# One line of 16 steps in the mixer, with each solve issued ahead of the last group's chain and heads

## The chip, the cores and the metric

The kernel runs on one core of a Trainium2 chip. The metric is the device time of one execution in microseconds; lower is better. The time before is 3080.9 us, the median of three runs (3077.79 to 3086.84).

## The reference

The reference is one decoder layer on 2048 tokens of width 1024, in float32. The part that matters here is the mixer. The normed input u is projected by w_in, and the columns go to two groups of heads, whose outputs are put side by side:

```python
u = rms_norm(h, norm_mix); z = u @ w_in
y_m = mlstm_group(z[..., :D_IN_MLSTM], ...)   # 4 heads of 128: conv, silu, chunkwise mLSTM in chunks of 128
y_r = rwkv7_group(z[..., D_IN_MLSTM:], ...)   # 8 heads of 64: a state S (64 x 64) per head, token by token:
#   sa = S a_t;  S = S * w_t + sa b_t + v_t k_t;  y_t = S r_t, then a norm, a bonus term and a gate
h = h + concat([y_m, y_r]) @ w_mix_out
```

After it come a cross-attention into 256 memory tokens, a SwiGLU feed-forward and a last norm. These stages are not touched.

## The kernel before

Every product of float32 values is made of three fp16 products (mm3: high times high, high times low, low times high), accumulated in PSUM. The scheduler of the language orders the instructions: each engine has a queue whose order is fixed when the program is built, by program order as priority and by a simulated time at which each instruction is ready; on the chip each queue runs in that order and waits at its head. A pool with bufs=n hands its n buffers of a tag round; a new tile waits for the last reader of the one whose buffer it takes. `tc.issue_after(ins)` queues what follows on the engine of `ins` behind it.

The mixer (mixer, mixer_pass) runs two passes, hq = 0 and 1, over half of the heads each: two pairs of RWKV heads (e = 0, 1, each 128 partitions wide) and two mLSTM heads. In a pass there are 8 groups (sg) of 256 tokens. A pass first loads and splits its weights: 8 RWKV tiles of three projections (wts[0], tag wh3) and 8 mLSTM tiles of four (wts[1], tag wh4), through wraw buffers of which there are two. Then, for each group:

- load_u: the group's u by DMA (4 tiles of each half, tags uh and ul; 8 buffers, so two groups).
- group: xw by DMA, and a set of buffers (MX, of which there are two; VX, bon and W, two each).
- prepare for e = 0, 1: wps, the projections kps, rps and vps, the decays and keys (KB, RR), the products aps with masks into MX, RR and AY, and the transposes kbps into KBt. bps gives bon, and a second matmul on vps (L385) gives the values VS. RR has four buffers, two groups. Its PSUM tiles come from pax (two banks) and pmm (two banks).
- solve: the triangular blocks of MX go to DRAM (md) and come back as M, and POOL inverts them in 31 steps of two operations (L434, L436). The result goes to DRAM (td, t1d) and comes back as T1 and into MX. Then PE joins the blocks: pps, an ACT copy, xps, an ACT copy into MX. pps and xps take the one bank of psx.
- scan: the state chain over 4 chunks (ch: three matmul stages with ACT copies between, and a DVE step into the next VS), and yps, the output. It returns a tail.
- the tail of the group before: the norm (dq, var, y), tps and gps in the bank of psx, yc, which adds bon and the gate, and the output by DMA.
- mlstm for e = 0, 1: qps twice, the convolution, vops, then skp, ncp and the state Cn; its tail (yt, ymps, ym) is run one head later. In the second pass the heads of the last two groups are held back to the end (late), and their u is loaded again.

Around it, pre_pass fills the first 100 us; after it memory_kv (kvps) and out_proj start as soon as their buffers come free.

Of the kernel before, what the change touches and what calls it, by code (L numbers as in the profile page):

```python
# [7 lines left out]
F32 = mybir.dt.float32  # L8
# [7 lines left out]
P = 128  # L16
# [18 lines left out]
Q0 = 2056  # L35
# [16 lines left out]
def mm3(nc, out, lhs, rhs, start, stop):  # L52
    nc.tensor.matmul(out, lhsT=lhs[0], rhs=rhs[0], start=start, stop=False)  # L53
    nc.tensor.matmul(out, lhsT=lhs[0], rhs=rhs[1], start=False, stop=False)  # L54
    nc.tensor.matmul(out, lhsT=lhs[1], rhs=rhs[0], start=False, stop=stop)  # L55

# [190 lines left out]
def mixer_pass(c, I, hq, tp, T):  # L247

    nc, tc = c.nc, c.tc
    SGN = 256  # L250
    NS = T // SGN
    w_in = I["w_in"][0]
# [3 lines left out]
    wts = [], []  # L256
    for n, o in ((3, Q0), (4, 0)):
        for k in range(KT):
            wk = w_in[k * P:(k + 1) * P, :]
            h = tp.w.tile([P, n * 2 * P], F16, tag=f"wh{n}", name="wh", bufs=8)  # L260
            l = tp.w.tile([P, n * 2 * P], F16, tag=f"wl{n}", name="wl", bufs=8)
            for j in range(0, n, 2):
                m = min(2, n - j)
                raw = tp.x.tile([P, 4 * P], F32, tag="wraw", name="wraw")[:, 0:2 * m * P]
                nc.sync.dma_start(raw.rearrange("p (j c) -> p j c", j=m),
                                  wk[:, o + 512 * j:o + 512 * (j + m)].rearrange("p (j c) -> p j c", j=m)[:, :, 2 * P * hq:2 * P * (hq + 1)])
                s = slice(2 * P * j, 2 * P * (j + m))
                split(nc, h[:, s], l[:, s], raw, c.gmix[:, k:k + 1])
            wts[n - 3].append((h, l))

    st = Ctx()
    st.VS = None
    st.Cn = []
    for e in range(2):
        st.Cn.append(tp.m2.tile([P, P + 1], F32, tag=f"Cn{e}", name="Cn"))
        nc.gpsimd.memset(st.Cn[e], 0.0)

# [13 lines left out]

    def values():
        return tp.sg.tile([P, 2, 4, 2, 64], F32, tag="VS", name="VS")

    def group(sg):
        G = Ctx()
        G.VS = st.VS
        if sg == 0:
            G.VS = values()
            for h in range(2):  # L300
                nc.gpsimd.memset(G.VS[halves[h], :, 0, h], 0.0)
        G.xw = (tp.t2.tile([P, 2, SGN], F16, tag="xw", name="xw"), tp.xz)
        x = [c.l_d[0][i].rearrange("(q p) t -> p q t", q=2)[:, :, sg * SGN:(sg + 1) * SGN] for i in range(2)]
        for b in halves:
            nc.sync.dma_start(G.xw[0][b], x[0])
        nc.sync.dma_start(G.xw[1][b0], x[1])
        G.MX = next(tp.MXs)
        G.VX = tp.sg.tile([P, 2, 4, 2, 64], F32, tag="VX", name="VX")
        G.bon = tp.sg.tile([P, 2, SGN], F32, tag="bon", name="bon")
        G.W = tp.sg.tile([P, 2, 4, 1], F32, tag="W", name="W")  # L310
        return G

    def prepare(sg, e, u, G):
# [10 lines left out]
        VS, VX = G.VS[:, e], G.VX[:, e]  # L324
# [6 lines left out]
        L = tp.t1.tile([P, SGN], F32, tag="L", name="L")  # L331
# [14 lines left out]
        ps = tp.pmm.tile([P, SGN + 1], F32, tag="mm", name="kps")  # L346
# [18 lines left out]
        for h, b in enumerate(halves):  # L365
            nc.vector.scalar_tensor_tensor(RR[b, :, h, 0:64], sq[b], c.kk[b, 0, ct:ct + 1], E[b, :, 0:64],
                                           op0=ALU.mult, op1=ALU.mult)
        kk = tp.t1.tile([P, SGN], F32, tag="kk", name="kk")
        nc.vector.scalar_tensor_tensor(kk, ta, 1.0, k, op0=ALU.add, op1=ALU.mult)
# [40 lines left out]
    def solve(MX, NG):  # L410
# [27 lines left out]
        for e in range(2):  # L438
            nc.sync.dma_start(td.rearrange("q h g u (c e) r -> e (q h g u) c r", e=2)[e], M[NB * e:NB * e + NB, 0:16])
            nc.sync.dma_start(t1d[e].rearrange("h g u r c -> (h g u) r c"), X[NB * e:NB * e + NB // 2])  # L440
        T1 = tp.t1.tile([P, NU, 32], F32, tag="T1", name="T1")
        for h in range(2):
# [8 lines left out]
        lohi = [(slice(64 * h, 64 * h + 32), slice(64 * h + 32, 64 * h + 64)) for h in range(2)]  # L451
        for i in range(NU):
            for h, (a, b) in enumerate(lohi):
                nc.tensor.matmul(pps[b, i], lhsT=MXu[a, i, h, 32:64], rhs=T1[a, i], start=True, stop=True)
        for a, b in lohi:
# [7 lines left out]

    def scan(sg, gs, G):
        y = tp.s2.tile([P, 2, 2, 2, 64], F32, tag="y", name="y")
        st.VS = values() if sg < NS - 1 else None
        for n in range(4):
            ch = tp.psc.tile([P, 2, 3, 64], F32, tag="ch", name="ch")
            for e, g in enumerate(gs):
                for h in range(2):  # L470
                    nc.tensor.matmul(ch[halves[h], e, 0], lhsT=g.RR[:, n, h, 0:64], rhs=G.VS[:, e, n, h], start=True, stop=True)
            R = tp.s2.tile([P, 2, 64], F32, tag="R", name="R")
            nc.scalar.copy(R, ch[:, :, 0])
            for e, g in enumerate(gs):
                nc.tensor.matmul(ch[:, e, 1], lhsT=g.M[:, n].rearrange("p h t -> p (h t)"), rhs=R[:, e], start=True, stop=True)
            for h, b in enumerate(halves):
                nc.scalar.copy(G.VX[b, :, n, h], ch[b, :, 1])
            for e, g in enumerate(gs):
                for h in range(2):
                    last = nc.tensor.matmul(ch[halves[h], e, 2], lhsT=g.KBt[:, n, h], rhs=G.VX[:, e, n, h], start=True, stop=True)  # L480
            dst = G.VS[:, :, n + 1] if n < 3 else st.VS[:, :, 0] if st.VS is not None else None
            if dst is None:
                break
            Sn = tp.s2.tile([P, 2, 64], F32, tag="Sn", name="Sn")
            for h, b in enumerate(halves):
                nc.vector.tensor_tensor(Sn[b], ch[b, :, 2], G.VS[b, :, n, h], ALU.add)
            for h, b in enumerate(halves):
                nc.vector.tensor_tensor(dst[b, :, h], Sn[b], G.W[b, :, n].to_broadcast([64, 2, 64]), ALU.mult)
# [47 lines left out]
    def mlstm(sg, e, u):  # L536
        t0 = sg * SGN
        hp = 2 * hq + e
        m2 = tp.m2
        mb = m2.tile([P, SGN], F32, tag="mb", name="mb")  # L540
        sb = m2.tile([P, SGN], F32, tag="sb", name="sb")
        for i, t in enumerate((mb, sb)):
            nc.sync.dma_start(t, c.m_d[i].rearrange("(h n) t -> h (n t)", h=4)[hp, t0:t0 + SGN].partition_broadcast(P))
        qk = m2.tile([P, 2, SGN], F32, tag="qk", name="qk", bufs=1)
        for j in range(2):
# [7 lines left out]
            for i in range(3):  # L553
                nc.vector.scalar_tensor_tensor(a, z[:, i:i + SGN], cw(i), a, op0=ALU.mult, op1=ALU.add)
            th = m2.tile([P, SGN], F32, tag="th", name="th")
            nc.scalar.activation(th, a, AF.Tanh, scale=0.5)
# [7 lines left out]
        for n in range(2):  # L564
            ts = slice(n * P + 4, (n + 1) * P + 4)
            for k in range(KT):
                h, l = wts[1][k]
                mm3(nc, ps[:, n], (u[k][0][:, ts], u[k][1][:, ts]),
                    [x.rearrange("p (j e d) -> p j e d", j=4, e=2)[:, 2:4, e] for x in (h, l)], k == 0, k == KT - 1)
# [26 lines left out]
        def tail():  # L596
# [5 lines left out]
            nc.vector.reciprocal(r, r)  # L602
            sq = m2.tile([P, 2, P], F32, tag="th", name="msq")
            ss = m2.tile([P, 2], F32, tag="ss", name="ss")
# [4 lines left out]
            nc.vector.scalar_tensor_tensor(r, r, 0.5 * SYM, ss, op0=ALU.mult, op1=ALU.mult)  # L609
            yt = m2.tile([P, 2, P], F32, tag="yt", name="yt", bufs=1)  # L610
            nc.vector.scalar_tensor_tensor(yt, tho, 1.0, num, op0=ALU.add, op1=ALU.mult)
# [24 lines left out]

    mtails, stails = [], []

    def run_mlstm(sg, u):
        for e in range(2):  # L640
            mtails.append(mlstm(sg, e, u))
            if len(mtails) > 1:
                mtails.pop(0)()

    late = []
    for sg in range(NS):
        u = load_u(sg)
        G = group(sg)
        gs = [prepare(sg, e, u, G) for e in range(2)]
        solve(G.MX, 2)  # L650
        stails.append(scan(sg, gs, G))
        if len(stails) > 1:
            stails.pop(0)()
        if hq == 1 and sg >= NS - 2:
            late.append(sg)
        else:
            run_mlstm(sg, u)
    for sg in late:
        run_mlstm(sg, load_u(sg))
    for t in stails + mtails:  # L660
        t()


def mixer(c, I, T):
    tc = c.tc
    with ExitStack() as ctx:
        tp = Ctx()
        for name, bufs, space in (("x", 2, None), ("w", 10, None), ("u", 8, None), ("t2", 1, None),
                                  ("t1", 1, None), ("m2", 2, None), ("k", 2, None), ("sl", 4, None), ("sg", 2, None), ("RR", 1, None), ("s2", 2, None), ("MX", 1, None), ("pmm", 2, PSUM),
# [15 lines left out]
        tc.nc.gpsimd.memset(tp.xz, 0.0)  # L685
        for hq in range(2):
            mixer_pass(c, I, hq, tp, T)

# [748 lines left out]
```

## Time and profile before

| what | us |
|---|---|
| median of 3 runs | 3080.9 |
| the profiled execution | 3079.7 |
| its span, first to last instruction | 3077.9 |
| PE busy | 2907.4 |
| DVE busy | 2099.1 |
| ACT busy | 1210.7 |
| POOL busy | 1143.2 |

The profile is of one execution. Times within it count from the first instruction, in us. PE is the matmul engine, DVE, ACT and POOL the vector, scalar and general engines, SP the queue that issues the DMAs. The 40 slices of the page are 77 us each; the mixer lies in slices 2 to 17. Busy time of PE counts matmuls that overlap one another once. In brackets at the end of a timeline row is the engine's idle time before it and what ended it. The granted clock is a share of 2.4 GHz: 1.00 is full, 0.50 is 1.2 GHz, and a mean over a stretch lies between.

### The profile page before, as it was taken

How to read it: one execution, taken by the hardware profiler on the slowest of the kernel's cores; microseconds unless marked ns; L12 is line 12 of the kernel's file. 1: busy time of each engine (PE TensorE's matmuls, PEld its weight loads, DVE VectorE, ACT ScalarE, POOL GpSimd, SP SyncE). 2: the span in 40 equal slices, each digit the busy share in tenths (PEclk: the TensorE clock that was granted, in tenths of full speed). 3: DMA queues.
4: the chain of work that ended last, by engine and by line, in shares of the span. 5: the costliest groups of instructions: out<-in, count | busy, mean ns of one | idle time of the engine just before them, and what ended most of it. 6: DMA issues, size and time to landing. Idle time of an engine off the chain costs nothing. (4 is left out here: it accounts for less than half of the span.)

```text
span 3077.9 us, 53602 instructions
## 1 busy us (share of the span) xinstructions
PE 2907.4 (94%) x20259; PEld 1806.3 (59%) x20259; DVE 2099.1 (68%) x3821; ACT 1210.7 (39%) x2763; POOL 1143.2 (37%) x1862
## 2 busy tenths in 40 slices
PE   7799999989999978999999999999999999899998
PEld 4588788778888867765455544444444444344443
DVE  5676677787777766665488897554445455897975
ACT  6444433454444434554366653222222222423332
POOL 2144555555445554033112234222222221644542
PEclk9899999999999988999999999999999999999999
DMA  8612211242122212564323356211111112554442
GB/s 270 143 48 51 55 47 44 57 124 52 47 62 52 52 45 84 179 201 148 110 86 124 109 203 212 73 58 55 55 55 55 59 59 63 178 188 145 155 141 76
DMA packets 333181, 309.34 MB, mean 101 GB/s; under 512 B 89102, under 2 KB 282876, under 8 KB 332028
## 3 DMA queue, kind: packets, MB, share of 16 engines
q1 hardware_dynamic: 332924, 305.94, 32.4%
q8 instruction: 159, 2.61, 0.3%
q14 instruction: 98, 0.80, 0.1%
HBM read 210.36 MB, written 95.49 MB: 99 GB/s over the span
## 5 line engine op out<-in xcount | busy, mean ns | idle before, releaser
L53 PE MATMUL pp<-u,wb 128*128 128x512 f16 x1232 | 467.5, 379 | 14.2 <-DVE e L1142 9.4
L54 PE MATMUL pp<-u,wb 128*128 128x512 f16 x1232 | 467.7, 380 | 0.0
L55 PE MATMUL pp<-u,wb 128*128 128x512 f16 x1232 | 467.3, 380 | 0.0
L1142 DVE TENSOR_TENSOR e<-pp,e 128x512 f32<-128x512 f32 x308 | 208.6, 689 | 303.1 <-PE pp L55 290.2
L55 PE MATMUL dps<-w,gS 128*128 128x512 f16 x616 | 233.4, 379 | 10.8 <-DVE gS L49 10.8
L54 PE MATMUL dps<-w,gS 128*128 128x512 f16 x616 | 233.5, 379 | 1.7 <-DVE w L49 1.7
L53 PE MATMUL dps<-w,gS 128*128 128x512 f16 x616 | 233.5, 379 | 0.0
L434 POOL TENSOR_TENSOR tmp<-M,X 64x126 f32<-64x126 f32 (+22 forms) x496 | 187.2, 377 | 116.3 <-DMA M<-md 82.7
L436 POOL TENSOR_TENSOR X<-X,tmp 64x126 f32<-64x126 f32 (+22 forms) x496 | 202.4, 408 | 35.7
L54 PEld LDWEIGHTS <-wb 128*128 128x128 f16 x1232 | 120.6, 98 | 156.3 <-issue 12.4
L53 PEld LDWEIGHTS <-wb 128*128 128x128 f16 x1232 | 120.7, 98 | 150.9 <-DMA u<-u_d 5.4
L55 PEld LDWEIGHTS <-wb 128*128 128x128 f16 x1232 | 120.7, 98 | 146.0 <-issue 0.7
L1158 POOL TENSOR_TENSOR S<-raw 128x512 f32<-128x512 f32 x22 | 33.0, 1500 | 413.7 <-DVE wb L49 413.7
L53 PE MATMUL vops<-wh,uh 128*128 128x256 f16 x512 | 144.5, 282 | 8.4 <-ACT cv L552 8.1
L53 PE MATMUL qps<-uh,wh 128*128 128x259 f16 x512 | 144.8, 283 | 4.6 <-ACT wh L48 2.8
L54 PEld LDWEIGHTS <-wh 128*128 128x128 f16 x1280 | 128.6, 101 | 28.6 <-issue 8.1
L55 PE MATMUL vops<-wh,ul 128*128 128x256 f16 x512 | 144.5, 282 | 0.0
L54 PE MATMUL vops<-wl,uh 128*128 128x256 f16 x512 | 144.1, 282 | 0.0
L55 PE MATMUL qps<-uh,wl 128*128 128x259 f16 x512 | 143.6, 282 | 0.2 <-DVE wl L49 0.2
L54 PE MATMUL qps<-ul,wh 128*128 128x259 f16 x512 | 143.7, 281 | 0.0
L53 PEld LDWEIGHTS <-wh 128*128 128x128 f16 x1280 | 127.6, 100 | 22.3 <-ACT wh L48 3.7
L55 PEld LDWEIGHTS <-wl 128*128 128x128 f16 x1280 | 127.2, 99 | 20.4 <-DVE wl L49 0.9
(420 smaller groups left out, 7657.3 us busy)
## 6 DMA issues: line engine op xcount, KB each, us to landing
g_d<-e SPq DMA_DIRECT2D x88, 256.0 KB
h<-h_d SPq DMA_DIRECT2D x32, 512.0 KB
acc<-h_d SPq DMA_DIRECT2D x32, 512.0 KB
u_d<-ub SPq DMA_DIRECT2D x56, 256.0 KB
wraw<-in_w_in_dram SPq DMA_DIRECT2D x48, 256.0 KB
ga<-g_d SPq DMA_DIRECT2D x32, 384.0 KB
raw<-in_ffn_w_gate_dram SPq DMA_DIRECT2D x22, 512.0 KB
raw<-in_ffn_w_up_dram SPq DMA_DIRECT2D x22, 512.0 KB
```

Source lines behind the costliest of these rows:

```text
L53: nc.tensor.matmul(out, lhsT=lhs[0], rhs=rhs[0], start=start, stop=False)
L54: nc.tensor.matmul(out, lhsT=lhs[0], rhs=rhs[1], start=False, stop=False)
L55: nc.tensor.matmul(out, lhsT=lhs[1], rhs=rhs[0], start=False, stop=stop)
L434: nc.gpsimd.tensor_tensor(tv, M[:, s, s + 1:32].unsqueeze(2).to_broadcast(shp), X[:, s, 0:ncl].unsqueeze(1).to_broadcast(shp), ALU.mult)
L436: nc.gpsimd.tensor_tensor(X[:, s + 1:32, 0:ncl], X[:, s + 1:32, 0:ncl], tv, ALU.add)
L1142: add = lambda o, x, y: nc.vector.tensor_tensor(o, x, y, ALU.add)
L1158: nc.gpsimd.tensor_tensor(s[0], a[1][0], a[1][1], ALU.add)
```

## The change

mixer_pass no longer runs its pass. It returns its parts, and mixer makes one line of 16 steps of the two passes. In step i a group is prepared; the join of group i-1 is issued; the solve of group i is issued up to its DMAs back to DRAM; then come the scan of group i-1, its first mLSTM head, its tail, and its second head. The solve is cut in two: solve (to td and t1d) and join (T1, MX, pps, xps). The pps matmuls of join(i-1) are queued behind the last vops matmul of mlstm(i-2). The RWKV weights of a pass are loaded ahead of its first preparation and the mLSTM weights after that step; u is loaded a step ahead, with 12 buffers. VS is allocated in group; a scan writes the next group's VS (NX). mb, sb, th and y go from two buffers to one, yt takes the tag of kt and kk that of L. The late heads are gone.

```diff
 def mm3(nc, out, lhs, rhs, start, stop):
...
-    nc.tensor.matmul(out, lhsT=lhs[1], rhs=rhs[0], start=False, stop=stop)
+    return nc.tensor.matmul(out, lhsT=lhs[1], rhs=rhs[0], start=False, stop=stop)
...
     wts = [], []
-    for n, o in ((3, Q0), (4, 0)):
+
+    def weights(i):
+        n, o = ((3, Q0), (4, 0))[i]
         for k in range(KT):
...
     def group(sg):
         G = Ctx()
-        G.VS = st.VS
+        G.VS = tp.sg.tile([P, 2, 4, 2, 64], F32, tag="VS", name="VS")
         if sg == 0:
-            G.VS = values()
...
-        kk = tp.t1.tile([P, SGN], F32, tag="kk", name="kk")
+        kk = tp.t1.tile([P, SGN], F32, tag="L", name="kk")
...
             nc.sync.dma_start(t1d[e].rearrange("h g u r c -> (h g u) r c"), X[NB * e:NB * e + NB // 2])
+        return MXu, NU, td, t1d
+
+    def join(MXu, NU, td, t1d, after):
+
         T1 = tp.t1.tile([P, NU, 32], F32, tag="T1", name="T1")
...
-        for i in range(NU):
-            for h, (a, b) in enumerate(lohi):
-                nc.tensor.matmul(pps[b, i], lhsT=MXu[a, i, h, 32:64], rhs=T1[a, i], start=True, stop=True)
+        with tc.issue_after(after.ins) if after is not None else nullcontext():
+            for i in range(NU):
+                for h, (a, b) in enumerate(lohi):
+                    nc.tensor.matmul(pps[b, i], lhsT=MXu[a, i, h, 32:64], rhs=T1[a, i], start=True, stop=True)
...
-    def scan(sg, gs, G):
-        y = tp.s2.tile([P, 2, 2, 2, 64], F32, tag="y", name="y")
-        st.VS = values() if sg < NS - 1 else None
+    def scan(sg, gs, G, NX):
+        y = tp.s2.tile([P, 2, 2, 2, 64], F32, tag="y", name="y", bufs=1)
...
-            dst = G.VS[:, :, n + 1] if n < 3 else st.VS[:, :, 0] if st.VS is not None else None
+            dst = G.VS[:, :, n + 1] if n < 3 else NX.VS[:, :, 0] if NX is not None else None
...
-        mb = m2.tile([P, SGN], F32, tag="mb", name="mb")
-        sb = m2.tile([P, SGN], F32, tag="sb", name="sb")
+        if sg == 0:
+            st.Cn[e] = m2.tile([P, P + 1], F32, tag=f"Cn{e}", name="Cn")
+            nc.gpsimd.memset(st.Cn[e], 0.0)
+        mb = m2.tile([P, SGN], F32, tag="mb", name="mb", bufs=1)
+        sb = m2.tile([P, SGN], F32, tag="sb", name="sb", bufs=1)
...
-            th = m2.tile([P, SGN], F32, tag="th", name="th")
+            th = m2.tile([P, SGN], F32, tag="th", name="th", bufs=1)
...
-                mm3(nc, ps[:, n], (u[k][0][:, ts], u[k][1][:, ts]),
+                st.last = mm3(nc, ps[:, n], (u[k][0][:, ts], u[k][1][:, ts]),
...
-            yt = m2.tile([P, 2, P], F32, tag="yt", name="yt", bufs=1)
+            yt = m2.tile([P, 2, P], F32, tag="kt", name="yt", bufs=1)
...
-    for sg in range(NS):
-        u = load_u(sg)
-        G = group(sg)
-        gs = [prepare(sg, e, u, G) for e in range(2)]
-        solve(G.MX, 2)
-        stails.append(scan(sg, gs, G))
-        if len(stails) > 1:
-            stails.pop(0)()
-        if hq == 1 and sg >= NS - 2:
-            late.append(sg)
-        else:
-            run_mlstm(sg, u)
-    for sg in late:
-        run_mlstm(sg, load_u(sg))
...
-        for hq in range(2):
-            mixer_pass(c, I, hq, tp, T)
+        NS = T // 256
+        steps = [(p, sg) for p in [mixer_pass(c, I, hq, tp, T) for hq in range(2)] for sg in range(NS)]
+        mtails, us, after = [], {}, None
+
+        def run(i, NX):
+
+            nonlocal after
+            p, sg = steps[i]
+            tail = p.scan(sg, gs[i], G[i], NX)
+            for e in range(2):
+                mtails.append(p.mlstm(sg, e, us[i]))
+                if e == 0:
+                    tail()
+                if len(mtails) > 1:
+                    mtails.pop(0)()
+            after = p.st.last
+
+        G, gs, tri = {}, {}, {}
+        for i, (p, sg) in enumerate(steps):
+            if sg == 0:
+                p.weights(0)
+            if i == 0:
+                us[0] = p.load_u(0)
+            if i + 1 < len(steps):
+                us[i + 1] = steps[i + 1][0].load_u(steps[i + 1][1])
+            G[i] = p.group(sg)
+            gs[i] = [p.prepare(sg, e, us[i], G[i]) for e in range(2)]
+            if i > 0:
+                p.join(*tri[i - 1], after)
+            tri[i] = p.solve(G[i].MX, 2)
+            if i > 0:
+                run(i - 1, G[i] if sg > 0 else None)
+            if sg == 0:
+                p.weights(1)
+        steps[-1][0].join(*tri[len(steps) - 1], after)
+        run(len(steps) - 1, None)
```

## Rows read from the trace of the kernel before

**Rows 1.** The page's first part: busy time of each engine, share, instructions.

```profile
PE 2907.4 (94%) x20259; PEld 1806.3 (59%) x20259; DVE 2099.1 (68%) x3821; ACT 1210.7 (39%) x2763; POOL 1143.2 (37%) x1862
```

**Rows 2.** The page's second part: PE's busy tenths in 40 slices.

```profile
PE   7799999989999978999999999999999999899998
```

**Rows 3.** Windows at groups' first projections: start, end, length, then busy time per engine.

```profile
core 0: us, PE busy (x) PEld busy (x) DVE busy (x) ACT busy (x) POOL busy (x), PEclk, DMA share, GB/s
377.00:445.00 68.00, 64.74 (x675) 55.46 (x674) 49.06 (x119) 27.85 (x85) 34.35 (x82) 0.95 0.21 50
511.00:577.00 66.00, 62.33 (x677) 54.01 (x677) 49.53 (x120) 27.89 (x86) 35.45 (x90) 1.00 0.21 53
577.00:651.00 74.00, 65.29 (x680) 55.88 (x679) 56.58 (x131) 37.33 (x99) 34.89 (x82) 0.98 0.35 87
651.00:724.00 73.00, 65.11 (x659) 54.09 (x657) 60.08 (x138) 37.64 (x103) 40.76 (x86) 0.98 0.40 102
308.00:1051.00 743.00, 695.18 (x7316) 598.01 (x7315) 556.86 (x1326) 323.85 (x955) 391.53 (x914) 0.98 0.24 59
```

**Rows 4.** PE's waits, 100 to 1300 us: total us, times, longest us.

```profile
PE pps L454 <- DMA T<-t1d: 43.4, 18, 6.2
PE wps L330 <- ACT KBt L407: 10.3, 9, 7.4
```

**Rows 5.** Timeline, 393 to 485 us: start, duration, engine, line, operation, tiles, count.

```profile
393.41 1.12 DVE L366 SCALAR_TENSOR_TENSOR RR<-sq,kk,E 64x256 f32<-64x256 f32 x2
...
417.34 0.31 PE L454 MATMUL pps<-T,MX 32*32 32x32 f32 x2 [2.38 <-DMA T<-t1d]
...
424.85 0.73 ACT L462 COPY MX<-xps 32x256 f32<-32x256 f32 x2 [1.87 <-PE xps L460]
...
428.12 0.61 PE L514 MATMUL tps<-ident,y 128*128 128x128 f32 x4
...
429.93 0.69 DVE L526 TENSOR_TENSOR yc<-yc,bon 128x512 f32<-128x512 f32 x1
...
431.69 0.42 DVE L382 TENSOR_TENSOR bon<-bps,v 128x256 f32<-128x256 f32 x1
...
432.14 0.47 ACT L288 ACTIVATE v<-vps,mu_c 128x256 f32<-128x256 f32 x1 [1.45 <-DVE bon L382]
...
440.90 0.43 DVE L399 TENSOR_TENSOR MX<-aps,mask 64x256 f32<-64x256 f32 x1
...
444.17 0.39 ACT L570 ACTIVATE vx<-vops 128x256 f32<-128x256 f32 x1
...
485.06 0.24 PE L454 MATMUL pps<-T,MX 32*32 32x32 f32 x2 [2.33 <-DMA T<-t1d]
```

**Rows 6.** Timeline, 491 to 530 us: the start and the end of group 4's chain.

```profile
491.14 0.73 ACT L462 COPY MX<-xps 32x256 f32<-32x256 f32 x2 [1.07 <-PE xps L460]
...
529.07 0.29 PE L495 MATMUL yps<-VS,RR 128*64 128x64 f32 x4
```

**Rows 7.** Windows at the start and at the end of the mixer.

```profile
100.00:181.00 81.00, 60.92 (x516) 48.99 (x513) 51.99 (x130) 37.29 (x85) 9.15 (x33) 0.83 0.44 89
1051.00:1240.00 189.00, 158.68 (x1615) 134.95 (x1614) 120.46 (x287) 74.09 (x216) 98.37 (x233) 0.87 0.28 75
```

**Rows 8.** Timeline of ACT and PE around 145 us.

```profile
144.35 0.72 ACT L48 ACTIVATE wh<-wraw,gmix 128x512 f16<-128x512 f32 x1 [8.17 <-DMA wraw<-in_w_in_dram]
...
145.89 0.37 PE L330 MATMUL wps<-xw,lwa 128*128 128x256 f16 x1 [7.44 <-ACT KBt L407]
```

**Rows 9.** Timeline of SP: the first load of u for group 1.

```profile
177.97 0.38 SPq L633 DMA_DIRECT2D uh<-u_d  x1
```

**Rows 10.** Waits of all engines, 236 to 1051 us.

```profile
ACT th L556 <- DVE cv L554: 31.2, 33, 3.2
...
ACT wh L48 <- DMA wraw<-in_w_in_dram: 28.9, 21, 3.7
```

**Rows 11.** Groups of PE instructions by line, 1229 to 1283 us: count, busy us, mean ns.

```profile
L54 PE MATMUL kvps<-memT,wk 128*128 128x256 f16 x128 | 35.6, 278 | 0.0
```

More of the change, by code (lines that the diff above doesn't have):

```diff
@@ L250, in mixer_pass @@
     SGN = 256
-    NS = T // SGN
     w_in = I["w_in"][0]
@@ L268, in mixer_pass @@
                 split(nc, h[:, s], l[:, s], raw, c.gmix[:, k:k + 1])
-            wts[n - 3].append((h, l))
+            wts[i].append((h, l))
     st = Ctx()
[L272 to L276, printed above, removed]
+    st.Cn = [None, None]
     def project(ps, j, e, u):
@@ L290, in shifted @@
         return o
-    def values():
-        return tp.sg.tile([P, 2, 4, 2, 64], F32, tag="VS", name="VS")
     def group(sg):
         G = Ctx()
-        G.VS = st.VS
+        G.VS = tp.sg.tile([P, 2, 4, 2, 64], F32, tag="VS", name="VS")
         if sg == 0:
-            G.VS = values()
             for h in range(2):
@@ L602, in tail @@
             nc.vector.reciprocal(r, r)
-            sq = m2.tile([P, 2, P], F32, tag="th", name="msq")
+            sq = m2.tile([P, 2, P], F32, tag="th", name="msq", bufs=1)
             ss = m2.tile([P, 2], F32, tag="ss", name="ss")
@@ L635, in load_u @@
         return u
[L637 to L645, printed above, removed]
-    for sg in range(NS):
-        u = load_u(sg)
-        G = group(sg)
-        gs = [prepare(sg, e, u, G) for e in range(2)]
-        solve(G.MX, 2)
-        stails.append(scan(sg, gs, G))
-        if len(stails) > 1:
-            stails.pop(0)()
-        if hq == 1 and sg >= NS - 2:
-            late.append(sg)
-        else:
-            run_mlstm(sg, u)
-    for sg in late:
-        run_mlstm(sg, load_u(sg))
-    for t in stails + mtails:
-        t()
+    p = Ctx()
+    p.weights, p.load_u, p.group, p.prepare, p.solve, p.join, p.scan, p.mlstm, p.st = \
+        weights, load_u, group, prepare, solve, join, scan, mlstm, st
+    return p
 def mixer(c, I, T):
@@ L667, in mixer @@
         tp = Ctx()
-        for name, bufs, space in (("x", 2, None), ("w", 10, None), ("u", 8, None), ("t2", 1, None),
+        for name, bufs, space in (("x", 2, None), ("w", 10, None), ("u", 12, None), ("t2", 1, None),
                                   ("t1", 1, None), ("m2", 2, None), ("k", 2, None), ("sl", 4, None), ("sg", 2, None), ("RR", 1, None), ("s2", 2, None), ("MX", 1, None), ("pmm", 2, PSUM),
@@ L685, in mixer @@
         tc.nc.gpsimd.memset(tp.xz, 0.0)
-        for hq in range(2):
-            mixer_pass(c, I, hq, tp, T)
+        NS = T // 256
[31 more added lines that the diff above has]
+        run(len(steps) - 1, None)
+        for t in mtails:
+            t()
 def out_proj(c, I, T):
```

## The prediction

> **What bounds the kernel now.** I read the page's first two parts, then the mixer cut into its steps, then what PE waited for, and last one turn of the largest wait. Every time below is made against the profiled execution: 3079.7 us, of which 1.8 lie around the span of 3077.9. The median of the runs is 1.2 above it.
>
> PE is busy for 94% of the span and no other engine for more than 68% [rows 1]. The slices show PE full from the 18th on, so only the mixer, from about 100 to 1285 us, has something to give [rows 2].
>
> Cut at the first projection of each group, a group away from the pass boundary takes 66 to 68 us. At clock 1.00 PE has 62.3 us of work in 66, at 0.95 it has 64.7 in 68; the two groups at the boundary take 74 and 73 [rows 3]. PE sets the pace, with some 3.5 us idle per group. Most of this has one owner: PE waits 43.4 us for T1, the solve's result that comes back by DMA. The next wait, wps with 10.3, belongs mostly to the start [rows 4].
>
> One turn of that wait [rows 5]. T1 of group 3 is there and pps starts at 417.34; ACT writes the joined MX at 424.85. Only then does tps of group 2's tail run, at 428.12: it takes the one psx bank, and the program gives it to pps and xps first. yc adds bon at 429.93, which frees that buffer, so group 4's bon is written at 431.69; this frees v, which ACT shifts for head 1 at 432.14. The last MX of the group follows at 440.90. The solve runs on POOL, and pps of group 4 finds T1 at 485.06. From pps to pps this is 67.7 us, one step. So each solve waits for the join of the solve before it: a loop through one step, beside a PE that has 62 us of work in it.
>
> **The change part by part.**
>
> *The order.* In the trace the chain of group 4 already runs from MX at 491.14 to yps at 529.07 [rows 6], that is beside the preparation of group 5 and the start of group 6, whose step begins at 511 [rows 3]. Much of the overlap that the new order writes out is there, made by the planner. New are two things. tail(i) is issued in its own step, ahead of the next join, so tps no longer stands behind that join on psx. And prepare(i) is ahead of scan(i-1) and mlstm(i-1).
>
> The loop through bon now spans two steps: last MX to pps 44.2 (485.06 - 440.90), pps to MX written 8.2 (425.58 - 417.34), chain 37 (491.9 to 529.1), yps to the release of bon, and from there to the last MX 10 (441.3 - 431). Of the fourth term tps to yc is 2.5; even 20 for it leaves 119 for two steps, 60 for one, below PE's 62.
>
> Another loop stays. RR, VS and MX have two sets, so RR of group i waits for the chain of group i-2. RR of head 0 at 393.41 to the last MX at 440.90 is 47.5 [rows 5]; with 44.2, 8.2 and 37 it makes 137 for two steps, 68 for one. The 47.5 hold the wait for bon, which goes; I expect 35, and so 62 for one step. This leaves no room to speak of below PE.
>
> *A. The wait at pps.* The last solve has nothing to hide behind, so of 18 gaps one of the mean size, 2.4, stays; at most -41 goes. At least nothing: pps is queued on PE where the planner believes T1 to be, the chip needs 44.2 us from the last MX, and the edge to the last vops of group i-2 moves pps only if that comes later. ACT takes group 4's last vops at 444.17, just as its preparation ends [rows 5]; with the heads a step later this lies beside the end of prepare(5), and T1 still needs its 44. The edge alone does not reach. I take half, -20, because the loop is cut but the place in PE's queue is not.
>
> *B. The clock.* The granted clock over the eleven groups from 308 to 1051 is 0.98, so 15 us of 743 [rows 3]; the lower steps have the longer gaps. Bounds 0 and -15; it goes with the waits, by half, -7.
>
> *C. The start.* From 100 to 181 PE is busy 60.9 of 81 at 0.83 [rows 7]: 20 idle, and up to 14 for the clock. ACT was held 8.17 by one weight load, and behind it stood the KBt copy and wps [rows 8]; u for group 1 was issued only at 177.97 [rows 9]. Now u(1) is loaded ahead, and prepare(1) is issued ahead of mlstm(0), whose weights come last. The first solve and chain still pass bare. Bounds 0 and -25; I take -12, near the 10.3 of wps plus part of the clock.
>
> *D. The pass boundary.* 147 us for two groups against 132: 15 too long [rows 3]. ACT waited 28.9 us for weight loads there [rows 10]. The RWKV weights can now load when prepare(7) is through, a step ahead of their use. The mLSTM weights still wait for mlstm(7), and are wanted after prepare(9) and the chain; with 16 loads that cover may be too short, and then PE stands as before. Bounds 0 and -15; -8.
>
> *E. The end.* From 1051 to 1240 PE is idle 30.3 of 189 at 0.87 [rows 7]. Before, the heads of groups 14 and 15 were held back for the last chains; now those of 14 lie beside solve(15), and those of 15 beside what is left, nearly the same. The last chain is covered by the kvps matmuls, of which one of three lines, 128 each, is at work for 35.6 us [rows 11]; they want the mLSTM weights out of the way. If the heads run out before solve(15) is back, up to +15 is bare; if the joins of 13 and 14 no longer stall, up to -25 goes. I take -6.
>
> *F. Fewer buffers.* mb, sb, th and y lose one, yt takes kt's, kk takes L's. The next mb is queued on SP behind the readers of the last one, and behind it on SP stand md, t1d and T1, which have more room than before. kt of the next head waits for the transposes of yt. Where a single buffer is handed round already, th from cv, ACT waits 31.2 us in 33 for it, off PE's path [rows 10]. Bounds 0 and +25, nearer the first; +4. The 16 reloads of u for the two held-back groups go, and nothing waited for them: 0. The memsets of Cn, VS allocated in group() and the return value of mm3 move beside a busy PE: 0. If that cover is gone, a memset or two at the start.
>
> Sum: -20 - 7 - 12 - 8 - 6 + 4 = -49. 3079.7 - 49 = 3030.7, and with the 1.2 to the median 3032.
>
> One rule speaks against the change. The Trainium skill, "Perfetto Trace Analysis", section Identifying the Most-Contended Engine, says that a gap which repeats on the engine that should be full can mean that there is too little SBUF or PSUM for the next tile. The change adds no PSUM bank and takes SBUF buffers away, so by this rule A and B would be nothing. The trace agrees by half: the wait ends on a DMA, but what makes the DMA late is the single psx bank.
>
> **The rivals.** *The wait stays* (24%). The planner had overlapped the chain already, and queues pps where it believes T1 to be; A and B are nothing, and the edges count: -12 - 8 - 6 + 4 = -22, so 3059. For it: the place of the chain in the trace, and 44 us from MX to pps as before. Against it: the loop through psx and bon is cut.
>
> *All of it goes* (11%): -41 - 15 - 20 - 13 - 12 + 4 = -97, so 2984. For it: the bon loop falls below PE's work. Against it: the RR loop near 62.
>
> *Slower* (12%). prepare(i) ahead of scan(i-1) stretches the chain, for which RR, VS and MX of group i+1 wait. At 68 per step this loop is as long as a step now. Each microsecond added to it costs half of one in each of some 13 steps, 6.5 in all. If head 0 to last MX does not shrink and the chain grows by 10, that is +65, and with the edges +43, so 3124. It decides from a net growth of 3.4 us (22 / 6.5). For it: 68 against 66. Against it: the 47.5 hold the wait for bon.
>
> *Nothing moves* (3%): the edges and new waits cancel, 3081.
>
> **How the numbers follow.** The forecast has 50%, with 3000 to 3060 as its own range. From 2985 to 3080 the range holds the forecast, nearly all of the first rival and half of the second; outside lie the other half of it and the slower case. A measurement of this kernel tells 0.3%, some 9 us, from no change. Faster: the forecast, 11% and 19 of the first rival's 24, 80% in all; the same: its other 5 and the 3, 8%; slower: 12%.
>
> **What would show it.** Right: PE's wait at pps falls from 43 to about 20; tps of a group starts ahead of the next group's pps; the last MX comes earlier in its step; steps of 63 to 65 us; the boundary's two groups below 140; PE busy for over 68 of the first 81 us. Wrong: pps waits 2.3 in each step as before (the first rival); or PE waits at ch, aps or kps for VS, RR or the copies, and steps are above 67 (the slower one).

## The result, and the profile after

The changed kernel takes 3048.6 us (median of 4 runs, 3046.7 to 3052.1), the kernel before 3083.9 beside it: ratio 0.9888, 95% interval 0.9867 to 0.9910, some 35 us faster. The forecast was 3032, with 3000 to 3060 as its own range: the direction came, and about two thirds of the gain. The wait that the change was to cut fell as forecast; the idle time of PE hardly did. The profiled execution is the slowest of the four, 3052.1 with a span of 3050.4, so the two profiles lie only 27.5 us apart; the accounts below add up to that. Of the six executions of b_tail below one took 6010.6 us, which no run explains; its median counts it, its ratio does not.

The page's first part and PE's slices, to be held against [rows 1, 2]:

```profile
PE 2888.4 (95%) x20259; PEld 1798.7 (59%) x20259; DVE 2097.6 (69%) x3821; ACT 1213.9 (40%) x2763; POOL 1134.6 (37%) x1862
PE   7779999998999998999999999999999999899998
```

PE's waits of after, 100 to 1300 us (total us, times, longest us), for [rows 4]:

```profile
PE qps L53 <- DVE r L286: 19.5, 13, 2.2
PE qps L53 <- ACT cv L552: 10.9, 13, 0.8
...
PE pps L452 <- DMA T<-t1d: 5.6, 3, 4.2
```

The wait for T1 fell from 43.4 to 5.6. But two waits at qps, the first projection of an mLSTM head, hold 30.4 now; before, they were below 5. Windows of after, cut as [rows 3] at groups' first projections (start, end, length, busy times, clock, DMA); the first three are steady groups (away from the pass boundary), the next three the boundary, the last the same eleven groups as 308 to 1051 before:

```profile
359.00:423.00 64.00, 61.33 (x669) 53.53 (x667) 48.36 (x119) 28.07 (x85) 33.52 (x82) 1.00 0.21 52
423.00:488.00 65.00, 61.68 (x673) 54.01 (x671) 49.12 (x119) 28.70 (x87) 34.32 (x84) 1.00 0.21 53
488.00:552.00 64.00, 60.92 (x666) 53.34 (x664) 48.40 (x118) 27.92 (x85) 34.32 (x86) 1.00 0.22 51
552.00:622.00 70.00, 64.31 (x651) 55.20 (x650) 54.48 (x127) 34.10 (x94) 34.37 (x83) 0.93 0.32 85
622.00:692.00 70.00, 64.85 (x697) 56.58 (x696) 52.27 (x129) 32.26 (x97) 37.99 (x91) 1.00 0.26 61
692.00:764.00 72.00, 63.74 (x653) 54.22 (x651) 56.12 (x127) 35.42 (x92) 37.09 (x79) 0.95 0.36 91
296.00:1022.00 726.00, 682.37 (x7318) 593.77 (x7317) 551.79 (x1326) 326.61 (x954) 381.87 (x911) 0.99 0.24 60
```

The eleven groups went from 743 to 726. Of these 17 us only 4 are idle time of PE (743 - 695.2 = 47.8 before, 43.6 now); 13 are busy time, of the same matmuls. By the granted clocks, 0.98 of 743 us and 0.99 of 726, the lower clock took some 15 us before and some 7 now (17 and 9 where the windows are cut finer). So some 8 of the 13 are the clock; the other 5 are busy time that no run explains.

The ends are to be taken together, since the line leaves work of the start for the end (2084 and 2064 matmuls before; 1845 and 2321 now). First two rows before, then two after:

```profile
60.00:308.00 248.00, 218.70 (x2084) 175.98 (x2083) 169.32 (x402) 114.07 (x295) 82.03 (x209) 0.92 0.38 95
1051.00:1283.00 232.00, 201.15 (x2064) 171.43 (x2063) 149.38 (x355) 101.37 (x283) 101.05 (x235) 0.90 0.33 92
```

```profile
60.00:296.00 236.00, 194.60 (x1845) 156.13 (x1844) 154.22 (x352) 104.43 (x258) 86.01 (x213) 0.89 0.38 98
1022.00:1257.00 235.00, 217.12 (x2321) 187.71 (x2319) 168.10 (x406) 112.66 (x321) 101.28 (x238) 0.97 0.31 86
```

Together 480 became 471, again not by idle time (60.2 and 59.3) but by busy time (419.9 and 411.7); by the clocks shown, the lower clock took some 43 us of them before and some 33 now. With the eleven groups this is 26 of the 27.5 us: 5 idle, 21 busy, and of these some 18 the clock.

One step of after, for [rows 5] (start, duration, engine, line, operation, tiles, count; in brackets the idle time before and its releaser). First the end of group 3's chain, beside the preparation of group 5:

```profile
442.31 0.63 DVE L313 MEMSET RR<- 64x256 f32 x2 [0.76 <-PE ch L468]
...
446.27 0.29 PE L492 MATMUL yps<-VS,RR 128*64 128x64 f32 x4
...
446.54 0.61 DVE L483 TENSOR_TENSOR Sn<-ch,VS 64x128 f32<-64x128 f32 x2 [2.11 <-ACT VX L474]
...
447.18 0.62 DVE L485 TENSOR_TENSOR VS<-Sn,W 64x128 f32<-64x128 f32 x2
...
447.83 0.96 DVE L371 TENSOR_TENSOR RR<-r,E 64x256 f32<-64x256 f32 x2
...
448.83 0.47 ACT L285 ACTIVATE r<-rps,mu_c 128x256 f32<-128x256 f32 x1 [2.90 <-DVE RR L371]
...
449.34 0.48 DVE L286 SCALAR_TENSOR_TENSOR r<-rps,mu_s,r 128x256 f32<-128x256 f32 x1 [0.54 <-ACT r L285]
...
449.87 0.27 PE L53 MATMUL qps<-uh,wh 128*128 128x259 f16 x1 [1.34 <-DVE r L286]
```

This is the new wait. RR of head 0 stands on DVE behind the chain's last step. It is the last reader of r, so ACT can't write the next r; rps keeps its bank, and qps, which is queued for that bank, stops PE for 1.34. The first row is the loop through RR of the prediction: RR of group 5 is not written before the chain of group 3 has read that part of the same buffer for the last time. Then the tail and the join:

```profile
454.74 1.64 POOL L506 TENSOR_TENSOR var<-var,mhalf 128x8 f32<-128x8 f32 x1
...
458.21 1.06 POOL L507 TENSOR_TENSOR y<-y,var 128x512 f32<-128x512 f32 x1
...
459.33 0.66 PE L511 MATMUL tps<-ident,y 128*128 128x128 f32 x4 [1.15 <-POOL y L507]
...
466.46 0.69 PE L452 MATMUL pps<-T,MX 32*32 32x32 f32 x32
```

tps of group 3 is now ahead of pps of group 4. pps comes 50.0 us after the last MX of its group (416.48), where the way through the solve took 44 before, and has nothing to wait for. In place of 2.4 us at pps the step has 1.34 here, 0.84 behind cv, and 1.15 at tps: 3.3 us of idle, as before the change.

### The profile page after: what moved, and what is told of

Same layout as the page of the kernel before. It is cut to its first block, busy times and chain, and to the rows that moved or that the text cites. A ratio compares the mean times of both kernels' runs of the same rounds, so it can differ in the third digit from the quotient of the medians.

```text
span 3050.4 us, 53575 instructions
## 1 busy us (share of the span) xinstructions
PE 2888.4 (95%) x20259; PEld 1798.7 (59%) x20259; DVE 2097.6 (69%) x3821; ACT 1213.9 (40%) x2763; POOL 1134.6 (37%) x1862
## 5 line engine op out<-in xcount | busy, mean ns | idle before, releaser
L1173 POOL TENSOR_TENSOR S<-raw 128x512 f32<-128x512 f32 x22 | 33.8, 1536 | 410.8 <-DVE wb L49 410.8
L53 PE MATMUL qps<-uh,wh 128*128 128x259 f16 x512 | 144.5, 282 | 30.4 <-DVE r L286 19.5
```

What stands on the lines that cost most here:

```text
L1173: nc.gpsimd.tensor_tensor(s[0], a[1][0], a[1][1], ALU.add)
```

## The experiments

Each kernel is made of the one before or of the changed one by the diff shown. The table has the median, the ratio to the kernel before with its interval, and for the same eleven groups of the profiled execution their length, PE's idle time in it, and the clock. The profiled execution of a_tailY is the slowest of its twelve, 3078.0.

| kernel | us | ratio | groups | idle | clock |
|---|---|---|---|---|---|
| before | 3077.6 to 3083.9 | 1 | 743 | 47.8 | 0.98 |
| after | 3048.6 | 0.9888 (0.9867 to 0.9910) | 726 | 43.6 | 0.99 |
| b_tail | 3020.9 | 0.9804 (0.9783 to 0.9824) | 694 | 21.4 | 1.00 |
| b_bon3 | 3055.9 | 0.9924 (0.9905 to 0.9942) | 733 | 43.7 | 0.98 |
| b_tail_one | 3044.3 | 0.9883 (0.9863 to 0.9903) | 722 | 33.8 | 0.98 |
| b_tail_wraw3 | 3023.4 | 0.9816 (0.9796 to 0.9836) | 702 | 23.9 | 0.99 |
| a_noedge | 3049.4 | 0.9904 (0.9887 to 0.9921) | 724 | 44.8 | 1.00 |
| a_tailY | 3069.2 | 0.9966 (0.9953 to 0.9979) | 745 | 42.4 | 0.97 |
| a_solvelate | 3054.2 | 0.9919 (0.9902 to 0.9935) | 731 | 47.2 | 0.99 |
| a_two | 3068.7 | 0.9964 (0.9948 to 0.9979) | 740 | 48.8 | 0.97 |
| a_mbsb | 3052.2 | 0.9911 (0.9898 to 0.9925) | 726 | 42.7 | 0.99 |
| a_ytth | 3053.4 | 0.9919 (0.9906 to 0.9933) | 724 | 41.0 | 0.99 |
| a_full8 | 3068.5 | 0.9965 (0.9953 to 0.9978) | 736 | 49.5 | 0.99 |
| a_half10 | 3065.1 | 0.9957 (0.9943 to 0.9971) | 735 | 48.7 | 0.99 |

**b_tail**: of the change, only this in the kernel before: a group's tail is issued after its own first mLSTM head, ahead of the next join.

```diff
             mtails.append(mlstm(sg, e, u))
+            if e == 0 and stails:
+                stails.pop(0)()
...
         stails.append(scan(sg, gs, G))
-        if len(stails) > 1:
-            stails.pop(0)()
```

> The kernel before with one thing of the change: a group's tail is issued behind its own first mLSTM head, ahead of the next group's join, in place of one group later behind that join. Theory (the one psx bank): this alone cuts the loop pps - MX - tps - bon - v - last MX - solve - pps; the wait at pps falls from 43 to under 20 and the time by 15 to 30, to 3054 to 3069. Rival (the gain comes from preparing a group and issuing its solve ahead of the last group's chain and heads): the wait stays at about 40 and the time within 6 us of the kernel before.

The eleven groups' window, and the head of PE's waits, 100 to 1300 us:

```profile
303.00:997.00 694.00, 672.63 (x7327) 588.28 (x7326) 552.73 (x1327) 321.74 (x956) 381.13 (x914) 1.00 0.26 63
```

```profile
PE pps L454 <- DMA T<-t1d: 11.9, 5, 4.4
```

And the largest of PE's waits in the eleven groups:

```profile
PE tps L514 <- POOL y L510: 5.5, 7, 1.8
```

This one move gives 60 us, more than the whole change. No wait takes the place of the one at pps within the groups; of the wait's 11.9 us, 11.0 lie behind them, at the end. In the groups tps of the tail runs ahead of the next pps here too, on the bank they share. A steady group takes 60 to 63 us. It is the fastest version of all, and it beats both kernels with intervals apart.

**b_bon3**: the kernel before with three bon buffers.

```diff
-        G.bon = tp.sg.tile([P, 2, SGN], F32, tag="bon", name="bon")
+        G.bon = tp.sg.tile([P, 2, SGN], F32, tag="bon", name="bon", bufs=3)
```

> The kernel before with three buffers for bon in place of two, order untouched. Theory (the loop runs through bon): group i's bon no longer waits for the tail of group i-2, v is free earlier, the last MX of a group comes some 10 us earlier in its step, the wait at pps falls to under 25 and the time by 10 to 25, to 3059 to 3074. Rival (bon's wait is beside the path, and PE's queue order alone makes the wait at pps): wait and time as in the kernel before, within 6 us.

```profile
PE pps L454 <- DMA T<-t1d: 23.8, 12, 3.1
```

With the tail still late, a third buffer alone takes 20 of the 43.4 off the wait and 24 us off the time. But only 10 of the 24 lie in the eleven groups, and there the wait goes on:

```profile
PE pps L454 <- DMA T<-t1d: 18.8, 8, 3.1
```

The last MX comes 56 us into its step (370.2 to 426.1) instead of 64, so the loop through bon is cut, and yet pps of that group is queued earlier too and waits 2.07 at 471.53. Room for bon shows the loop; the early tail shows that it is the order on the bank of psx that ends the wait in steady groups.

**a_tailY**: the changed kernel with tps and gps in the bank of yps instead of psx.

```diff
-            tps = tp.psx.tile([P, 2, SGN], F32, tag="sx", name="tps")
+            tps = tp.psc.tile([P, 2, SGN], F32, tag="Y", name="tps")
...
-        gps = tp.psx.tile([P, 2, SGN], F32, tag="sx", name="gps")
+        gps = tp.psc.tile([P, 2, SGN], F32, tag="Y", name="gps")
```

> The kernel after with the tail's tps and gps in the bank of yps, which is free between two groups, in place of psx. Theory (the one psx bank): in the kernel after the steps of 64.3 us are a loop chain - tail - psx free - pps - xps - chain (yps of group 3 at 448, tps 459.3, gps read at 463.6, pps 466.5, MX 472.6, yps of group 4 at 512), while PE has 61 us of work in a step; T1 has landed some 8 us before pps starts. Without the bank between them pps starts when T1 is there, steps go to 61.5 to 63 and the time to 3015 to 3032. A part may come back as a wait of pps for T1 of 1 to 2 us a step. Rival (PE's work with its short waits sets 64.3): no change, 3043 to 3053.

Slower by 20 to 24 (by medians or by ratios), where I expected faster or the same. The waits, 100 to 1300 us:

```profile
PE pps L452 <- DMA T<-t1d: 33.6, 19, 4.3
```

Freed of the shared bank, pps is queued on PE ahead of the tail in some turns (398.77, with tps at 406.38) and waits there for T1; I read this as the place where the planner believes T1 to be, too early for the chip. In the change it is psx, given to tps and gps of the group before, that puts pps behind them, past the landing of T1. The loss is not idle time in the groups, though (42.4, and 43.6 in the change): their busy time is 20 us longer, at a clock of 0.97.

**a_noedge** (`after = None`, so pps isn't tied to the last vops) and **a_solvelate** (solve(i) issued behind run(i-1)) undo one edit of the line each:

```diff
-            tri[i] = p.solve(G[i].MX, 2)
             if i > 0:
                 run(i - 1, G[i] if sg > 0 else None)
+            tri[i] = p.solve(G[i].MX, 2)
```

> The kernel after without the edge that queues pps behind the last vops of the group before last. Theory (the one psx bank): in the kernel after pps of group 4 starts at 466.46, 43 us behind the last vops of group 3 (423), and right behind the tail of group 3, whose tps and gps hold the bank; so the edge is idle and the time stays within 5 us of the kernel after, 3043 to 3053, with a wait at pps of some 6 us in all. Rival (the edge is what keeps pps from waiting): the wait at pps comes back with 2 to 2.5 us a step, over 30 us in all, and the time is 3070 to 3085.

> The kernel after with the solve of group i issued behind the scan, heads and tail of group i-1 in place of ahead of them; all else as in the kernel after. Theory (the tail's POOL operations stand behind the solve's): in the kernel after var of group 3 is ready at 452.7 and its power runs on POOL at 454.74, behind the copies and the memset of solve 4, and an affine_select of 1.78 lies between it and the y product; so yps to tps takes 11.3 us (448.0 to 459.3) against 8 in the kernel before with the early tail, and the loop chain - tail - psx - pps - chain is 64.3 in place of 61. With the solve behind, steps go to 61 to 62.5 and the time to 3010 to 3030. Rival (the single buffers, or preparing ahead of the chain, cost the kernel after its 28 us against the early tail alone): 3043 to 3053 as before the edit.

Neither moves the time clear of the noise. The edge is idle (the last vops of group 3 ends at 423, pps of group 4 starts at 466). a_solvelate does not settle its theory, that the tail's POOL operations stand behind the solve's: in its profile POOL's queue is still in that order, with the solve's affine_select still between the tail's power (386.35) and its product, and yps to tps takes 12 us as before the edit (379.39 to 391.21; 382.29 to 394.33 in the change):

```profile
387.96 1.78 POOL L421 TENSOR_SCALAR_AFFINE_SELECT X<-X 32x512 f32<-32x512 f32 x2
389.82 1.06 POOL L507 TENSOR_TENSOR y<-y,var 128x512 f32<-128x512 f32 x1
```

**a_two**: the changed kernel with the line cut at the pass boundary, so that group 7 is joined and run before group 8 is prepared.

```diff
+            if sg == 0 and i > 0:
+                steps[i - 1][0].join(*tri[i - 1], after)
+                run(i - 1, None)
             if sg == 0:
                 p.weights(0)
...
-            if i > 0:
+            if sg > 0:
```

> The kernel after with its line cut at the pass boundary: join and scan, heads and tail of group 7 are issued ahead of the second pass's weights and of the preparation of group 8. Theory (the line hides nothing at the boundary: the three groups there take 74, 65 and 73 us in the kernel after, 19 over three steps of 64.3, and waiting for weights is the cause, whatever the order): within 10 us of the kernel after, 3043 to 3058. Rival (the line hides solve and chain of group 7 behind group 8): 20 to 40 us slower, 3068 to 3090.

Three groups at the boundary, first here, then in the change:

```profile
554.00:776.00 222.00, 197.73 (x1983) 168.59 (x1980) 162.24 (x380) 101.12 (x281) 110.18 (x251) 0.93 0.31 76
```

```profile
552.00:764.00 212.00, 192.90 (x1996) 166.00 (x1995) 162.87 (x382) 101.78 (x282) 109.45 (x252) 0.96 0.31 80
```

It costs 20 to 23. In the profiles, 17 us apart, 10 lie at the boundary and 4 in the other eight groups. So the theory, that the line hides nothing there, fell. In this order the line is needed at the boundary; against the kernel before, whose three groups take 208, it gains nothing there.

**b_tail_one** and **b_tail_wraw3**: b_tail with the change's single buffers (y aside), and with three wraw buffers.

```diff
-        mb = m2.tile([P, SGN], F32, tag="mb", name="mb")
+        mb = m2.tile([P, SGN], F32, tag="mb", name="mb", bufs=1)
...
-            yt = m2.tile([P, 2, P], F32, tag="yt", name="yt", bufs=1)
+            yt = m2.tile([P, 2, P], F32, tag="kt", name="yt", bufs=1)
...
```

> The kernel before with the early tail (3021) and with the change's single buffers: mb, sb, th one each, yt in kt's place, kk in L's. Theory (fewer buffers cost next to nothing): 3019 to 3029. Rival (the fewer buffers are what makes the kernel after slower than the early tail alone): 3038 to 3050.

> The kernel before with the early tail (3021) and three buffers for the raw weights in place of two. Theory (start and boundary wait for the weight loads, two in flight at a time): ACT's wait for wraw falls by a third, the two groups at the boundary, 67 and 74 us against 61, come near 63 to 68, and the time is 3005 to 3016. Rival (the loads' own rate, or the splits on ACT and DVE, set it): 3017 to 3026.

The buffers cost 24 us in this order; more room for the weights gives nothing. 12 of the 28 us that the groups lose are idle time of PE, 16 busy time, most of it the clock (0.98 of 722 us, 14).

**a_mbsb**, **a_ytth**, **a_full8**, **a_half10**: the buffers given back to the changed kernel, in two parts, and together. All together need room: a_full8 has 8 u tiles and loads u behind run(i-1); a_half10 has 10, y single, and loads half of u early.

```diff
-        mb = m2.tile([P, SGN], F32, tag="mb", name="mb", bufs=1)
-        sb = m2.tile([P, SGN], F32, tag="sb", name="sb", bufs=1)
+        mb = m2.tile([P, SGN], F32, tag="mb", name="mb")
+        sb = m2.tile([P, SGN], F32, tag="sb", name="sb")
...
-            if i + 1 < len(steps):
-                us[i + 1] = steps[i + 1][0].load_u(steps[i + 1][1])
```

> The changed kernel with two buffers each for mb and sb alone, the mLSTM head's rows that SP loads. Theory A: these are the single buffers that cost (SP's queue stands 70 us behind their readers in eight steps): half or more of the 24 us come back, 3022-3037. Theory B: the cost is in th, yt and kk: 3043-3053.

> The changed kernel with two th buffers and yt in a tile of its own instead of kt's. Theory A (mb and sb cost): 3043-3053. Theory B (ACT and DVE wait for each other over th and kt, between one head's end and the next group's start): half or more of the 24 us come back, 3022-3037.

> The changed kernel with every buffer of before restored (mb, sb, th, y two each; yt and kk in tiles of their own), paid for by 8 instead of 12 u tiles, so the loads of group i+1's u are issued behind run(i-1) instead of ahead of prepare(i). Theory: the single buffers cost about 24 us here as they do in the kernel of before with the early tail; steps fall from 64.3 to 62-63 us and the time to 3015-3035. Rival 1: what holds this kernel at 64 us a step is its order (a group prepared ahead, banks in another order), not the buffers: 3042-3055. Rival 2: u arrives late by 4 tiles less, and PE waits for u at the head of each prepare: over 3060.

> The changed kernel with two buffers each for mb, sb and th and tiles of their own for yt and kk (y stays single), paid for by 10 instead of 12 u tiles: half of u of the next group is loaded a step ahead as in the change, the other half behind run(i-1), so that u is late by little. Theory: in the 16-step line the order holds a step at 64 us, by three short waits of PE that come back in every step (qps behind r and behind cv, tps behind y, 3.3 us in one step); the buffers cost nothing there, and the time is 3042-3053. Rival: the single buffers cost about 24 us here as they do in the kernel of before with the early tail, and the time of 3068 with all of them restored was u being late: 3020-3035, with steps of 62-63. Third: u is still late, over 3055, with PE waits at kps for u as there (13 us).

The parts give nothing back, and all together are slower by 17 to 24 (by medians or by ratios). PE's waits in the eleven groups, a_full8 and then a_half10:

```profile
PE qps L53 <- DVE r L286: 10.9, 7, 2.0
...
PE kps L54 <- DMA ul<-u_d: 5.3, 8, 1.6
PE kps L53 <- DMA uh<-u_d: 5.2, 5, 2.3
```

```profile
PE qps L53 <- DVE r L286: 12.3, 8, 2.2
```

In a_full8 u is late (10.5 us at kps). In a_half10 kps waits 0.9 us for u in all, yet its time is the third case's: the time without its reason. The waits at qps stay in both. So in the line's order mb and sb by themselves, and th, yt by themselves, are not what holds a group at 64 us; all buffers at once were only tried together with later loads of u. Why the buffers and later loads together cost that much stays open.

## Why the prediction was right and where it was wrong

**A, the wait at pps (-20, bounds 0 and -41).** The loop through psx and bon is there, and the early tail cuts it: b_tail and b_bon3 show it, and the last MX now comes 57 us into its step (359 to 416.5) instead of 64. The half that I kept back because "the place in PE's queue is not" cut went too, by an accident that I didn't see: the same bank that made the loop now orders pps behind the tail. The step that failed is the next one. The wait fell by 38 in all, but I took this for time, and PE's idle time in the eleven groups fell by 4. The wait at pps in these groups, before and after:

```profile
PE pps L454 <- DMA T<-t1d: 26.5, 11, 5.5
```

```profile
PE pps L452 <- DMA T<-t1d: 1.2, 1, 1.2
```

Late next are the reader of a pmm bank that qps is queued for, and POOL's y; PE's waits of after in the same groups:

```profile
PE qps L53 <- DVE r L286: 15.2, 10, 2.2
PE qps L53 <- ACT cv L552: 8.4, 10, 0.8
PE tps L511 <- POOL y L507: 3.9, 4, 1.1
PE aps L388 <- DVE AY L394: 3.5, 1, 3.5
```

I had named ch, aps and kps as waits of the slower case, and none for the likely one. b_tail shows that they come of the line's order: there RR stands behind the same chain step on DVE, but PE has vps queued at that place and not qps. This is read from the traces; no run moved qps alone.

What sets the 64 us of a step is open, and two rivals stand untested. One is the loop through RR (below). The other goes once round per step: yps, the tail, psx, pps, the chain, and the next yps. From yps of group 3 to its tps it takes 13.1 us in the change (446.27 to 459.33); in b_tail, whose steps are 3 to 4 us shorter, it takes 10.2:

```profile
446.83 0.29 PE L495 MATMUL yps<-VS,RR 128*64 128x64 f32 x4
...
456.98 0.66 PE L514 MATMUL tps<-ident,y 128*128 128x128 f32 x4 [0.30 <-POOL y L510]
```

a_solvelate was to shorten this way and did not; a_tailY cut it at psx, but pps waited again.

**B, the clock (-7, bounds 0 and -15).** -8 in the eleven groups, so the size was right, and another -10 at the ends, which C and E held: in all the clock carries most of the gain. I had it go with the waits, by half. The wait at pps went almost wholly, the idle time hardly, and what the groups still lose to the clock lies at the boundary; all others are at 1.00 now. That "the lower steps have the longer gaps" holds in part only: of two groups with a wait of 2.4 at pps, one has 0.95 and one 1.00 (last section).

**C and E, start and end (-12 and -6).** The start alone looks right, 248 to 236, but it is work put off: with the end it is -9 of -18, and only 1 us of it idle time. The test that I set, PE busy for over 68 of 81 us from 100, failed:

```profile
100.00:181.00 81.00, 53.45 (x451) 42.59 (x448) 52.82 (x126) 36.98 (x79) 15.82 (x42) 0.79 0.41 92
```

**D, the pass boundary (-8).** The two groups from 552 take 140 instead of 147, not below the 140 that I set, and the third, 72, pays it back: 212 against 208 (577 to 785 before):

```profile
577.00:785.00 208.00, 189.69 (x1980) 162.18 (x1979) 163.09 (x374) 102.34 (x283) 113.16 (x260) 0.98 0.32 81
```

So the boundary cost 4, and the eight other groups gave 21, from 535 to 514. The doubt was stated: the mLSTM weights come late, now in the third group. ACT waits for weight loads as before, 27.0 against 28.9 [rows 10], 14.0 of it in the third group.

**F, fewer buffers (+4, bound +25).** In the line, 0 for each part that was tried. In b_tail's order the same buffers, y aside, cost 24, near the upper bound. The price belongs to the order in which they are used.

**The rivals.** *The wait stays* fell at pps, but its time, 3059, is nearer to the 3049 measured than the forecast's 3032. That the range held is in part luck: it was wide enough for both. The eleven groups brought 17 of the 35 of A, B and D together, the ends 9 of the 18 of C and E; F's 4 were not paid, and 5 of the 17 are busy time for which the sum has no term. *Slower* saw the loop through RR at 62 to 68 a step. It did not make steps of 68, but it is there in the change: in the eleven groups DVE waits ten times at RR for the chain,

```profile
DVE RR L313 <- PE ch L468: 9.3, 10, 1.4
```

which it does once in b_tail's and not before. Whether a third set of RR would shorten the step, no run tried. b_tail_one, without the line, and the change, with it, are within 4 us: line, preparing ahead and early loads of u bring together next to nothing beside the tail's move.

**The rule of the Trainium skill** ("Perfetto Trace Analysis", in its section Optimization Strategy, not the one that the prediction names: a repeated gap can mean too little SBUF or PSUM for the next tile) agrees with b_bon3 (one buffer more, -24) and b_tail_one (some fewer, +24). But with no buffer added b_tail gives 60: here the order in which one bank is handed on counts for more than room.

## What to carry to other kernels

A wait that ends last is worth its time only if PE has ready work queued at the place where it stood; so after pricing a wait, cut the idle time of the stretch and ask which instruction is late next. A bank that two chains share orders them on an in-order queue, for good or ill: try the smallest swap by itself before the large rebuild. Price a buffer that is given up in the order that will use it.

## What the runs showed of the hardware that was not expected

In these rows the size of a gap does not tell whether the clock falls behind it. In the kernel before, the 2.38 us wait at pps [rows 5] ends a stretch with 5.56 of 8 us busy, and in the next 8 us the granted clock is 0.58, most of it at the 1.2 GHz level. Two turns later the wait at pps is 2.37 (551.39), behind much the same work of all engines, and the clock stays at 2.4 GHz:

```profile
409.00:417.00 8.00, 5.56 (x48) 4.45 (x46) 6.45 (x12) 4.06 (x13) 5.70 (x12) 1.00 0.22 31
417.00:425.00 8.00, 7.66 (x89) 5.88 (x90) 4.13 (x10) 1.98 (x6) 0.92 (x1) 0.58 0.27 59
...
543.00:551.00 8.00, 5.61 (x49) 4.52 (x46) 6.45 (x12) 4.06 (x13) 5.69 (x13) 1.00 0.22 31
551.00:559.00 8.00, 7.20 (x108) 6.05 (x109) 6.46 (x15) 2.56 (x7) 0.92 (x1) 1.00 0.29 62
```

So it is with waits of 2.33 at 485.06 (lower behind it) and of 2.76 at 960.74 and 2.35 at 1025.53 (full). It also falls behind short gaps, here the longest of 0.99 us, at 674:

```profile
676.00:680.00 4.00, 3.53 (x18) 2.81 (x18) 3.94 (x10) 1.65 (x7) 3.75 (x8) 0.57 0.29 81
```

The step of after has 5.83 of 8 busy at its worst, idle in gaps of 1.34 and 0.84 us, and stays at 2.4 GHz, as does every group of the eleven away from the boundary:

```profile
448.00:456.00 8.00, 5.83 (x66) 5.10 (x61) 5.65 (x12) 3.05 (x9) 6.51 (x18) 1.00 0.15 25
```

So the same idle time can cost differently: a_tailY has no more of it than the change (42.4 and 43.6), but with the waits at pps back its clock is 0.97, and its groups take 745. What decides in a single turn stays open.
